# Weight sums of 41 of the 44 gate and value groups: accumulating DMAs in place of additions on VectorE and GpSimd

## The chip, the cores and the metric

One core of one Trainium2 chip runs the whole program. The core has a matrix engine (TensorE, PE in the profile, whose weight loads are the row PEld), VectorE (DVE), ScalarE (ACT), GpSimd (POOL) and SyncE (SP), and 16 DMA engines that move data between device memory (HBM) and on-chip memory (SBUF). Matmul results land in PSUM, which the DMA engines of this kernel never write. The metric is the device time of one execution in microseconds (us).

## The reference, cut to what matters

One decoder layer on 512 positions of width 2048: a hybrid of block-sparse attention and a state-space scan, an output projection, and a gated feed-forward block. The change lies in the feed-forward block:

```python
h = rms_norm(x, norm2_w)
u = causal_dwconv(h @ w_up, ffn_conv_w, ffn_conv_b)     # 2048 -> 2 * 5632, conv over 3 positions
u_gate, u_val = jnp.split(u, 2, axis=-1)
return x + (jax.nn.silu(u_gate) * u_val) @ w_down       # 5632 -> 2048
```

All arrays are float32. 5632 is 44 x 128, so there are 44 groups, each with 128 gate channels and the 128 value channels that belong to them.

## The kernel before

**Products.** Every matmul works on numbers split into a high and a low part (fp32r tiles `hi` and `lo`, ScalarE copies the high part, VectorE subtracts it to get the low part), and a product of two such numbers is three matmuls: hi x hi, hi x lo and lo x hi. The feed-forward products use a 2x2 block scheme with seven block products instead of eight, P1 to P7. A group's weights are four pieces of 128 x 1024 floats (512 KB each), named "11", "12", "21" and "22". Three of the seven products take a piece as it is (P1: 11, P2: 12, P4: 22, loaded a second time as "22b"); the other four take sums of pieces:

- T1 for P5: 21 and 22 added (`add` step s1, VectorE, line 1034)
- T2 for P6: T1 with 11 subtracted (s2, VectorE, line 1038)
- T4 for P3: 12 with T2 subtracted (s4, VectorE, line 1040)
- T3 for P7: 11 with 21 subtracted (s3, GpSimd, line 1027)

T1, T2 and T4 follow one another in place in one tile, the chain (`s`, in PSUM, two buffers). T3 is made in place in the tile that holds 21 (`rawb`, two buffers). The other pieces go into `rawa` (four buffers). The activations are combined in the same manner once (`sums`), and the results of the seven products are combined by `up_after` (first phase, "up", 44 groups) or `down_after` (second phase, "down", 24 groups in three passes of 7, 8 and 7 k-blocks).

**Order.** `items` is the list of products. Group g takes seven slots in the order P5(g), P3(g-1), P1(g), P4(g-1), P6(g), P2(g), P7(g). In the up phase an item is 24 matmuls of 128 x 256. Everything else hangs on slots: `at(slot, fn)` puts a step before or (`where=after`) after the low-part split of a slot, so the order on each engine is written out by hand. At slot k the kernel emits the matmuls of item k, then what reads their result, then the low part of item k+2 (`split_lo`, line 1060, two `lo2` buffers) and the high part of item k+3 (`split`, line 1051, three `hi2` buffers). ScalarE and VectorE work their queues in order; SP works the loads in order.

**Special items.** In groups 1, 2, 4, 15 and 30, and in three groups of each down pass, P3 is multiplied in another order and against a second copy of one activation tile (`twin`, line 1309). The result is the same.

**Ends of the phase.** The up phase starts when the output projection's last columns (`g_x2`) have been summed, and the scale 1/rms (`rstd`, a power on GpSimd at slot 3, transposed on TensorE at slot 4) is made during its first slots. From the last up group on, VectorE and ScalarE also split the gated activations that come back from HBM (`b_split`, lines 1106 and 1107) for the down phase. The gated activations of two up groups are collected in one tile `gt` and written by one DMA (line 1067, `gd<-gt`).

Of the kernel before, what the change touches and what calls it, by code (L numbers as in the profile page):

```python
# [20 lines left out]
F32 = mybir.dt.float32  # L21
# [3 lines left out]
OP = mybir.AluOpType  # L25
# [162 lines left out]
def body(ctx, tc, xT, wi, wz, wo, wu, wd0, wd1, wd2, pp, pf, outT, dbg={}):  # L188
# [697 lines left out]
    def sums(E, g, part=None):  # L886

        if part != 1:
            E.tensor_tensor(g[:, 4:6, :], g[:, 1:4:2, :], g[:, 0:2, :], op=OP.subtract)
        if part != 0:  # L890
            E.tensor_tensor(g[:, 6, :], g[:, 3, :], g[:, 4, :], op=OP.subtract)
            E.tensor_tensor(g[:, 7, :], g[:, 2, :], g[:, 6, :], op=OP.subtract)
# [121 lines left out]

    def load(gi, name):
        if name == "21":
            r = lp.tile([128, 1024], F32, name="rawb", bufs=2)
        else:
            r = lp.tile([128, 1024], F32, name="rawa", bufs=4)
        sy.dma_start(r[:, :cols(gi)], groups[gi]["src"][name[:2]])  # L1020
        raw[gi, name] = r

    def add(gi, name):
        n = cols(gi)
        if name == "s3":
            r = raw[gi, "21"][:, :n]
            po.tensor_tensor(r, raw[gi, "11"][:, :n], r, op=OP.subtract)  # L1027
            return
# [8 lines left out]
        if name == "s2":  # L1037
            ve.tensor_tensor(s_, s_, raw[gi, "11"][:, :n], op=OP.subtract)
        else:
            ve.tensor_tensor(s_, raw[gi, "12"][:, :n], s_, op=OP.subtract)  # L1040
# [28 lines left out]
    for gi in range(len(groups)):  # L1069
        p5, p1 = pos[gi, "P5"], pos[gi, "P1"]  # L1070
        p6 = pos[gi, "P6"]
        at(p5 - 8, load, gi, "21"), at(p5 - 8, load, gi, "22")
        at(p1 - 7, load, gi, "11"), at(pos[gi, "P2"] - 7, load, gi, "12"), at(pos[gi, "P4"] - 6, load, gi, "22b")
        if gi:
# [89 lines left out]
    def down_after(g, x):  # L1164
# [3 lines left out]
                              "P7": (X[:, lo], 1, hi, OP.add), "P4": (X[:, lo], 1, lo, OP.add),  # L1168
                              "P5": (X[:, hi], 1, hi, OP.add), "P3": (X[:, hi], 0, hi, OP.add),
# [3 lines left out]
        ve.tensor_tensor(a[:, row, half], src, a[:, row, half], op=op)  # L1173
# [9 lines left out]
    def up_after(g, x):  # L1183
# [9 lines left out]
        elif x == "P3":  # L1193
            ve.tensor_tensor(ug[:, 258:514], X[:, 256:], g["P6"], op=OP.add)
        else:
            ve.tensor_tensor(uv[:, 2:258], X[:, :256], rbc[:, :256], op=OP.mult)
            up_side(i, ug, uv)

    def up_side(i, ug, uv):
# [28 lines left out]
        for d, fn in ((0, lambda: ve.tensor_tensor(ug[:, 2:514], ug[:, 2:514], rbc, op=OP.mult)),  # L1228
                      (1, lambda: ve.tensor_tensor(uv[:, 258:514], uv[:, 258:514], rbc[:, 256:], op=OP.mult)),
# [119 lines left out]
```

## Time and profile before

| what | value |
|---|---|
| time, median of 2 runs | 2087.6 us (2086.79 to 2088.41) |
| span of the profiled execution, first to last instruction | 2086.9 us |
| profiled execution's time by the page | its span; the median run is 0.7 us above it |
| TensorE busy over the span | 98% |
| VectorE, ScalarE, GpSimd busy | 76%, 48%, 10% |
| DMA traffic | 328.18 MB, mean 157 GB/s |
| up phase | about 780 us to 1615 us |

A row of the windows view gives, for a stretch of time, each engine's busy time and instruction count, the granted TensorE clock, the mean busy share of the 16 DMA engines and the rate at which they moved bytes. A row of the groups by line gives the source line, the engine, the operation, result and operands, the form, the count, then total busy time and the mean in nanoseconds of one. A row of the timeline gives start, duration, engine, line, and in brackets how long the engine had idled and what released it. A row of the waits gives total, count and longest.

### The profile page before, as it was taken

To read this page: it belongs to the slowest core of one execution; us is meant where nothing else is said; L and a number is where in the kernel's file an instruction comes from. 1 tells how busy PE (TensorE), PEld (TensorE's weight loads), DVE (VectorE), ACT (ScalarE), POOL (GpSimd) and SP (SyncE) were. 2 spreads that over 40 slices of the span, in tenths; PEclk is the share of its full clock that TensorE was granted. 3 is DMA by queue.
4 is the path that set the end of the run, shared out by engine and by line. 5 is a ranking of instruction groups with operands and counts; after the bars stand their busy time and mean duration, and the time that the engine had idled before them with its cause. 6 is when DMAs were issued, how large, how long until landed. Compare 5 with 4: busy or idle time off the path is not lost.

```text
span 2086.9 us, 37696 instructions
## 1 busy us (share of the span) xinstructions
PE 2048.4 (98%) x15366; PEld 1934.0 (93%) x15366; DVE 1581.2 (76%) x2251; ACT 994.9 (48%) x1437; POOL 208.1 (10%) x107
## 2 busy tenths in 40 slices
PE   9999999999999998999999999999999899999999
PEld 8888888888888878999999999999999799899999
DVE  6545555345565557999999999999999977977976
ACT  6433435244445435555555555555555634534533
POOL 0020000000000001111110111011101111101110
PEclk9999999999999999999999999999999999999999
DMA  5233222332225545445444544454446667856763
GB/s 196 76 114 95 71 73 80 97 106 81 82 71 166 165 142 188 160 143 192 162 159 165 172 172 163 151 192 152 156 178 212 208 220 243 276 186 234 264 202 122
DMA packets 114396, 328.18 MB, mean 157 GB/s; under 512 B 10736, under 2 KB 35120, under 8 KB 111408
## 3 DMA queue, kind: packets, MB, share of 16 engines
q1 hardware_dynamic: 114224, 325.78, 46.4%
q8 instruction: 120, 1.97, 0.4%
q14 instruction: 52, 0.43, 0.1%
HBM read 283.77 MB, written 41.98 MB: 156 GB/s over the span
## 4 chain that ended last, share of the span: by engine, by line
PE 90%; DVE 6%; issue 1%; DMA 1%; ACT 1%; SPq 0%; DVEq 0%; POOL 0%; ACTq 0%; POOLq 0%
PE acc L183 30%; PE x L1320 15%; PE x L1317 15%; PE x L1318 15%; PE sm L183 4%; PE y L1317 3%; PE y L1320 3%; PE y L1318 3%; PE x L1309 2%; DVE lo L1060 2%; DVE cmb L1107 1%; DVE acc L1173 0%; DMA ld<-gd 0%; DVE s L1034 0%; DVE lo L183 0%
## 5 line engine op out<-in xcount | busy, mean ns | idle before, releaser
L1317 PE MATMUL x<-cmb,hi 128*128 128x256 f32 x3062 | 720.4, 278 | 12.4 <-ACT cP L1188 5.4
L1318 PE MATMUL x<-cmb,hi 128*128 128x256 f32 x3062 | 720.4, 278 | 11.6 <-DVE cmb L1107 11.6
L1317 PEld LDWEIGHTS x<-cmb,hi 128*128 128x128 f32 x3062 | 577.3, 189 | 14.9 <-issue 8.4
L1318 PEld LDWEIGHTS x<-cmb,hi 128*128 128x128 f32 x3062 | 577.4, 189 | 14.4 <-DVE cmb L1107 14.2
L1320 PE MATMUL x<-cmb,lo 128*128 128x256 f32 x3062 | 414.3, 277 | 1.0 <-DVE lo L1060 0.9
L1320 PEld LDWEIGHTS x<-cmb,lo 128*128 128x128 f32 x3062 | 379.0, 189 | 1.8 <-DVE lo L1060 1.8
L183 DVE TENSOR_TENSOR lo<-raw,hi 128x512 fp32r<-128x512 f32 (+1 forms) x240 | 164.4, 691 | 234.6 <-ACT hi L183 218.4
L1051 ACT ACTIVATE hi<-s 128x1024 fp32r<-128x1024 f32 (+1 forms) x201 | 201.1, 1000 | 284.6 <-DVE s L1034 186.1
L1027 POOL TENSOR_TENSOR rawb<-rawa,rawb 128x1024 f32<-128x1024 f32 (+1 forms) x68 | 169.9, 2498 | 1288.1 <-DVE s L1034 1087.6
L183 PE MATMUL acc<-A,hi 128*128 128x512 f32 x704 | 279.2, 397 | 0.8 <-ACT hi L183 0.8
L183 PE MATMUL acc<-A,lo 128*128 128x512 f32 x704 | 275.4, 391 | 0.0
L183 PE MATMUL acc<-B,hi 128*128 128x512 f32 x704 | 274.9, 391 | 0.0
L183 ACT ACTIVATE hi<-raw 128x512 fp32r<-128x512 f32 (+1 forms) x240 | 149.2, 629 | 247.5 <-PE acc L183 212.2
L1060 DVE TENSOR_TENSOR lo<-s,hi 128x1024 fp32r<-128x1024 f32 (+1 forms) x201 | 238.3, 1186 | 15.4 <-issue 13.2
L1060 DVE TENSOR_TENSOR lo<-rawa,hi 128x1024 fp32r<-128x1024 f32 (+1 forms) x204 | 241.5, 1184 | 4.2 <-PE x L1320 4.2
L1051 ACT ACTIVATE hi<-rawa 128x1024 fp32r<-128x1024 f32 (+1 forms) x204 | 209.6, 1028 | 37.1 <-PE x L1318 36.9
L183 PEld LDWEIGHTS acc<-A,lo 128*128 128x128 f32 x704 | 132.5, 188 | 28.8 <-DVE lo L183 0.6
L183 PEld LDWEIGHTS acc<-A,hi 128*128 128x128 f32 x704 | 132.9, 189 | 26.7 <-ACT hi L183 1.0
L183 PEld LDWEIGHTS acc<-B,hi 128*128 128x128 f32 x704 | 132.8, 189 | 26.0
L1188 ACT ACTIVATE cP<-x 128x256 f32<-128x256 f32 x132 | 50.7, 384 | 204.9 <-PE x L1320 204.9
L183 PE MATMUL acc<-hi,A 128*128 128x256 f32 (+2 forms) x448 | 134.6, 300 | 0.7 <-DVE u L183 0.7
L183 PE MATMUL acc<-hi,B 128*128 128x256 f32 (+2 forms) x448 | 132.7, 296 | 0.0
(211 smaller groups left out, 2865.2 us busy)
## 6 DMA issues: line engine op xcount, KB each, us to landing
rawa<-wu SPq DMA_DIRECT2D x176, 512.0 KB, 3.6
raw<-wi SPq DMA_DIRECT2D x79, 512.0 KB, 3.6
rawa<-wd SPq DMA_DIRECT2D x64, 448.0 KB, 4.3
rawb<-wu SPq DMA_DIRECT2D x44, 512.0 KB, 4.6
gd<-gt SPq DMA_DIRECT2D x22, 1024.0 KB, 4.5
raw<-wo SPq DMA_DIRECT2D x32, 512.0 KB, 3.5
rawa<-wd SPq DMA_DIRECT2D x32, 512.0 KB, 4.5
ld<-gd SPq DMA_DIRECT2D x27, 512.0 KB, 6.4
```

Of the source, the lines that this page charges most:

```text
L183: return fn(out, *args, **kw)
L1027: po.tensor_tensor(r, raw[gi, "11"][:, :n], r, op=OP.subtract)
L1051: se.activation(h[:, :n], src[:, :n], AF.Copy)
L1060: ve.tensor_tensor(l[:, :n], src[:, :n], h[:, :n].bitcast(F32), op=OP.subtract)
L1107: ve.tensor_tensor(lo, ld[:, :m, :], hi.bitcast(F32), op=OP.subtract)
L1188: se.activation(g[x], X[:, 256:] if x == "P5" else X[:, :256], AF.Copy)
L1309: pe.matmul(out, a[:, q * 128:(q + 1) * 128], b[:, q, :], start=False, stop=last and q == n - 1, skip_group_check=True)
L1317: pe.matmul(out, w, bk[:, 0, q, :], start=fresh and q == 0, stop=False, skip_group_check=True)
L1318: pe.matmul(out, w, bk[:, 1, q, :], start=False, stop=False, skip_group_check=True)
L1320: pe.matmul(out, l[:, q * 128:(q + 1) * 128], bk[:, 0, q, :], start=False, stop=q == n - 1, skip_group_check=True)
```

## The change

For groups 1 to 41 (`by_dma`) none of the four sums is made by an engine any more. SP loads 21 into the chain, and GpSimd issues a DMA that reads 22 from HBM and adds it to what is in the chain (`accum_op=OP.add`): that is T1. The same way 11 is added to the chain for T2 and 12 for T4. For T3, SP loads 21 a second time, into `rawb`, and GpSimd's DMA adds 11 to it. The chain of these groups lies in SBUF (`acc_s`, two buffers), since a DMA is to write it. Groups 0, 42 and 43 and the down phase keep the additions on VectorE and GpSimd.

An accumulating DMA adds, so all sums have to be additions. With 21 and 22 taken with turned sign, every subtraction of the scheme becomes an addition; the turned sign is carried by the activation sums (`sums`: three of the four outputs are formed in another way, two of them with a scalar-tensor-tensor instruction) and taken out of the results (`down_after` subtracts three products, `up_after` and `up_side` multiply the value half by -1 along with the scale).

```diff
         if part != 1:
-            E.tensor_tensor(g[:, 4:6, :], g[:, 1:4:2, :], g[:, 0:2, :], op=OP.subtract)
+            E.tensor_tensor(g[:, 4:6, :], g[:, 0:4:3, :], g[:, 1:2, :].to_broadcast([128, 2, 256]), op=OP.subtract)
         if part != 0:
-            E.tensor_tensor(g[:, 6, :], g[:, 3, :], g[:, 4, :], op=OP.subtract)
-            E.tensor_tensor(g[:, 7, :], g[:, 2, :], g[:, 6, :], op=OP.subtract)
+            E.scalar_tensor_tensor(g[:, 6, :], g[:, 4, :], -1.0, g[:, 3, :], op0=OP.mult, op1=OP.subtract)
+            E.scalar_tensor_tensor(g[:, 7, :], g[:, 6, :], -1.0, g[:, 2, :], op0=OP.mult, op1=OP.subtract)
...
+    by_dma = lambda gi: 0 < gi < NF - 2
+
+    def summed(gi, name):
+
+        d = groups[gi]["src"]
+        if name == "t1":
+            chain[gi] = lp.tile([128, 1024], F32, name="acc_s", bufs=2)
+            sy.dma_start(chain[gi], d["21"])
+            po.dma_start(chain[gi], d["22"], accum_op=OP.add)
+        elif name == "t3":
+            raw[gi, "21"] = lp.tile([128, 1024], F32, name="rawb", bufs=2)
+            sy.dma_start(raw[gi, "21"], d["21"])
+            po.dma_start(raw[gi, "21"], d["11"], accum_op=OP.add)
+        else:
+            po.dma_start(chain[gi], d["11" if name == "t2" else "12"], accum_op=OP.add)
+
...
-        at(p5 - 8, load, gi, "21"), at(p5 - 8, load, gi, "22")
+        if by_dma(gi):
+            at(p5 - 8, summed, gi, "t1"), at(p5 - 3, summed, gi, "t3")
+            at(p5 - 2, summed, gi, "t2", where=after), at(p6 - 2, summed, gi, "t4", where=after)
+        else:
+            at(p5 - 8, load, gi, "21"), at(p5 - 8, load, gi, "22")
         at(p1 - 7, load, gi, "11"), at(pos[gi, "P2"] - 7, load, gi, "12"), at(pos[gi, "P4"] - 6, load, gi, "22b")
+        if by_dma(gi):
+            continue
...
-            ve.tensor_tensor(uv[:, 2:258], X[:, :256], rbc[:, :256], op=OP.mult)
+            ve.scalar_tensor_tensor(uv[:, 2:258], X[:, :256], -1.0, rbc[:, :256], op0=OP.mult, op1=OP.mult)
             up_side(i, ug, uv)
...
-                      (1, lambda: ve.tensor_tensor(uv[:, 258:514], uv[:, 258:514], rbc[:, 256:], op=OP.mult)),
+                      (1, lambda: ve.scalar_tensor_tensor(uv[:, 258:514], uv[:, 258:514], -1.0, rbc[:, 256:],
+                                                           op0=OP.mult, op1=OP.mult)),
```

How the queues change is seen best in what stands in them. First GpSimd's queue at the start of the up phase, before (`rawb_7072` is group 0, `rawb_7082` group 1, and so on; `rstd` is the scale):

```order
L183 TENSOR_TENSOR rk_5572<-rk_5572,nhalf_134 128x4
L1027 TENSOR_TENSOR rawb_7072<-rawa_7076,rawb_7072 128x1024
L1027 TENSOR_TENSOR rawb_7082<-rawa_7166,rawb_7082 128x1024
L183 TENSOR_TENSOR rstd_132<-rstd_132,nhalf_134 128x4
L1027 TENSOR_TENSOR rawb_7309<-rawa_7420,rawb_7309 128x1024
L1027 TENSOR_TENSOR rawb_7550<-rawa_7653,rawb_7550 128x1024
```

The same place in the changed kernel (`acc_s_7082` is the chain of group 1, `acc_s_7309` of group 2, `acc_s_7549` of group 3; line 1023 makes T1, line 1029 T2 and T4, line 1027 T3):

```order
L183 TENSOR_TENSOR rk_5572<-rk_5572,nhalf_134 128x4
L1023 DMA acc_s_7082<-wu 128x1024
L1043 TENSOR_TENSOR rawb_7072<-rawa_7076,rawb_7072 128x1024
L1027 DMA rawb_7230<-wu 128x1024
L183 TENSOR_TENSOR rstd_132<-rstd_132,nhalf_134 128x4
L1029 DMA acc_s_7082<-wu 128x1024
L1023 DMA acc_s_7309<-wu 128x1024
L1029 DMA acc_s_7082<-wu 128x1024
L1027 DMA rawb_7483<-wu 128x1024
L1029 DMA acc_s_7309<-wu 128x1024
L1023 DMA acc_s_7549<-wu 128x1024
L1029 DMA acc_s_7309<-wu 128x1024
```

One instruction a group has become four, and their steady order is T2 of a group, T1 of the next, T4 of the group, T3 of the next. Two of them now stand ahead of the power that makes `rstd`.

Second, VectorE's queue about the P5 of an up group in mid-phase, before (`s_8908` is the chain of the group that begins, `s_8672` that of the group that ends, `lo2` the low parts):

```order
L889 TENSOR_TENSOR gt_8608<-gt_8608 128x512
L1228 TENSOR_TENSOR ug0_7150<-ug0_7150,rbc_131 128x512
L1060 TENSOR_TENSOR lo2_8906<-rawb_8497,hi2_8876 128x1024
L1034 TENSOR_TENSOR s_8908<-rawb_8736,rawa_8738 128x1024
L1229 TENSOR_TENSOR uv0_7152<-uv0_7152,rbc_131 128x256
L1190 TENSOR_TENSOR ug1_7154<-y_8914,cP1_8837 128x256
L1040 TENSOR_TENSOR s_8672<-rawa_8705,s_8672 128x1024
L1060 TENSOR_TENSOR lo2_8943<-s_8908,hi2_8912 128x1024
L1192 TENSOR_TENSOR uv1_7156<-x_8747,cP5_8772 128x256
L1060 TENSOR_TENSOR lo2_8976<-s_8672,hi2_8945 128x1024
```

The same place in the changed kernel:

```order
L889 TENSOR_TENSOR gt_8602<-gt_8602 128x512
L1250 TENSOR_TENSOR ug0_7149<-ug0_7149,rbc_131 128x512
L1076 TENSOR_TENSOR lo2_8902<-rawb_8664,hi2_8869 128x1024
L1251 SCALAR_TENSOR_TENSOR uv0_7151<-uv0_7151,rbc_131 128x256
L1212 TENSOR_TENSOR ug1_7153<-y_8907,cP1_8829 128x256
L1076 TENSOR_TENSOR lo2_8935<-acc_s_8730,hi2_8905 128x1024
L1214 TENSOR_TENSOR uv1_7155<-x_8740,cP5_8765 128x256
L1076 TENSOR_TENSOR lo2_8968<-acc_s_8492,hi2_8938 128x1024
```

The two 128 x 1024 additions between the low parts are gone (a third, line 1038, is gone a few rows further on), and the low parts read the chain from SBUF. On SP a group has five loads as before, with one of 22 replaced by a second one of 21; the load into the chain has to wait until the low part of P3 of the group two before has been read out of that buffer.

More of the change, by code (lines that the diff above doesn't have):

```diff
@@ L1026, in add @@
             r = raw[gi, "21"][:, :n]
-            po.tensor_tensor(r, raw[gi, "11"][:, :n], r, op=OP.subtract)
+            po.tensor_tensor(r, raw[gi, "11"][:, :n], r, op=OP.add)
             return
@@ L1037, in add @@
         if name == "s2":
-            ve.tensor_tensor(s_, s_, raw[gi, "11"][:, :n], op=OP.subtract)
+            ve.tensor_tensor(s_, s_, raw[gi, "11"][:, :n], op=OP.add)
         else:
-            ve.tensor_tensor(s_, raw[gi, "12"][:, :n], s_, op=OP.subtract)
+            ve.tensor_tensor(s_, raw[gi, "12"][:, :n], s_, op=OP.add)
     SOURCE = {"P1": "11", "P2": "12", "P4": "22b", "P7": "21"}
@@ L1167, in down_after @@
         src, row, half, op = {"P1": (X[:, lo], 0, lo, OP.add), "P6": (X[:, lo], 0, hi, OP.add),
-                              "P7": (X[:, lo], 1, hi, OP.add), "P4": (X[:, lo], 1, lo, OP.add),
-                              "P5": (X[:, hi], 1, hi, OP.add), "P3": (X[:, hi], 0, hi, OP.add),
+                              "P7": (X[:, lo], 1, hi, OP.subtract), "P4": (X[:, lo], 1, lo, OP.subtract),
+                              "P5": (X[:, hi], 1, hi, OP.subtract), "P3": (X[:, hi], 0, hi, OP.add),
                               "P2": (g.get("Y"), 0, lo, OP.add)}[x]
@@ L1172, in down_after @@
             src = src[:, lo]
-        ve.tensor_tensor(a[:, row, half], src, a[:, row, half], op=op)
+        ve.tensor_tensor(a[:, row, half], a[:, row, half], src, op=op)
         if g is groups[-1]:
```

## The prediction

> **What bounds the kernel now.** I read the page's busy row first, then the windows by stage, then the waits.
>
> ```profile
> span 2086.9 us, 37696 instructions
> PE 2048.4 (98%) x15366; PEld 1934.0 (93%) x15366; DVE 1581.2 (76%) x2251; ACT 994.9 (48%) x1437; POOL 208.1 (10%) x107
> ```
> ```profile
> 780.00:790.00 10.00, 4.76 (x24) 4.48 (x24) 8.63 (x13) 4.19 (x9) 2.38 (x1) 0.76 0.75 265
> ...
> 800.00:1000.00 200.00, 200.00 (x1753) 200.00 (x1754) 186.33 (x229) 109.66 (x139) 27.69 (x12) 1.00 0.46 162
> 1000.00:1200.00 200.00, 200.00 (x1766) 200.00 (x1765) 189.30 (x236) 106.81 (x138) 24.65 (x10) 1.00 0.48 166
> ...
> 1400.00:1600.00 200.00, 200.00 (x1767) 200.00 (x1766) 190.07 (x239) 106.73 (x138) 24.64 (x10) 1.00 0.50 174
> 1600.00:1800.00 200.00, 184.68 (x1562) 180.82 (x1561) 173.97 (x222) 97.65 (x110) 27.34 (x11) 0.99 0.70 236
> ```
> ```profile
> POOL rawb L1027 <- DVE s L1034: 1087.6, 66, 21.7
> ...
> PE x L1318 <- DVE cmb L1107: 11.6, 13, 2.3
> ...
> PE x L1317 <- ACT cP L1188: 5.4, 2, 5.0
> ```
>
> TensorE is idle for 2086.9 - 2048.4 = 38.5 us in all, and for none of it between 800 and 1600 us, where groups 1 to 41 run. There VectorE is 93 to 95% busy (186.33 to 190.07 of 200), close behind but never waited for. What TensorE loses in the up and down phases lies at the start (5.2 us of 780:790) and at the handover to the down phase (15.3 us of 1600:1800), where it waits for the split of gated activations (`cmb`, line 1107). DMA is at half load (0.48, 166 GB/s in the second of these rows), GpSimd sits and waits.
>
> So the most any change could win without touching the matmuls is 38.5 us, 1.8% of the median. Differences of over 2% (41.8 us) are what a measurement of this kernel can surely tell from no change: faster by that much is out of reach here.
>
> **What the change removes.**
>
> ```profile
> L1034 DVE TENSOR_TENSOR s<-rawb,rawa 128x1024 f32<-128x1024 f32 x51 | 62.5, 1226 | 0.0
> L1038 DVE TENSOR_TENSOR s<-s,rawa 128x1024 f32<-128x1024 f32 x51 | 62.5, 1225 | 0.0
> L1040 DVE TENSOR_TENSOR s<-rawa,s 128x1024 f32<-128x1024 f32 x51 | 62.2, 1219 | 0.0
> L1027 POOL TENSOR_TENSOR rawb<-rawa,rawb 128x1024 f32<-128x1024 f32 x52 | 130.4, 2507 | 1030.7 <-DVE s L1034 847.1 <-DVE gx L183 183.6
> ```
>
> Per group VectorE loses 1.226 + 1.225 + 1.219 = 3.67 us, over 41 groups 150 us; GpSimd loses 41 x 2.507 = 103 us. All of it lies beside a TensorE that has no gap. On the path: 0. At the handover VectorE does bind, but groups 42 to 45, whose sums fall into it, keep their additions, so nothing is won there either, unless VectorE enters it with a backlog. It does not: with 5% idle just before (190.07 of 200), it is caught up.
>
> **The signs.** Two 256-column and, for each pair of groups, two more 256-column operations on VectorE become scalar-tensor-tensor.
>
> ```profile
> L1207 DVE SCALAR_TENSOR_TENSOR tg<-ug,par,tg 128x512 f32<-128x512 f32 x88 | 65.6, 745 | 0.8 <-ACT tg L1206 0.8
> ...
> L1218 DVE TENSOR_TENSOR gt<-tg,tv 128x512 f32<-128x512 f32 x44 | 30.4, 691 | 1.5
> ```
>
> That costs 745 - 691 = 54 ns at 512 columns, 27 to 54 ns at 256: at most 3 x 0.054 = 0.16 us a group, against 3.67 us freed. On the path only the two of the last activation sum before the up phase: 0.1 us.
>
> **What it adds: DMA bytes.** A group moved six 512 KB units: five loads and half of a 1 MB write of gated activations (166 GB/s x 19.04 us = 6.0 units; 19.04 us is the step between the last two PE rows but two below). Now it is six and four accumulating ones. What a unit costs under pressure I take from the busiest stretch with TensorE full:
>
> ```profile
> 1596.00:1604.00 8.00, 8.00 (x73) 8.00 (x72) 7.13 (x10) 3.05 (x5) 0.00 (x0) 1.00 1.08 369
> ```
>
> 369 GB/s makes 1.42 us a unit. No row shows an accumulating DMA; call its weight w units. Then the engines need (6 + 4w) x 1.42 us of every 19.04, which fits up to w = 1.85. From below w = 1, a plain load (14.2 us, 75%). From above I bound it at w = 3 (fetch, fetch again, write, with no overlap): 25.6 us, 6.5 us over, x 41 = 267 us. I take a value under 1.85, nearer to the plain load, since the bytes written are the same and the second operand comes from on-chip memory.
>
> The Trainium skill, page "Collectives: The Full Stack", section "The bandwidth ceiling: the fold count and why AG ≠ RS ≠ AR", speaks against that: an add in the DMA path needs two source reads, and a reducing transfer ran at 1/1.93 of a copying one. No run here has shown it yet; by w = 1.93 the engines' need would be 19.5 us, 0.44 over, 18 us in all.
>
> **What it adds: latency.** An addition was 1.2 us in the queue of the engine that needed it; now a DMA has to be issued and land between one use of the chain and the next.
>
> ```profile
> rawa<-wu SPq DMA_DIRECT2D x176, 512.0 KB, 3.6
> ...
> rawb<-wu SPq DMA_DIRECT2D x44, 512.0 KB, 4.6
> ...
> ld<-gd SPq DMA_DIRECT2D x27, 512.0 KB, 6.4
> ```
> ```profile
> 1016.09 1.22 DVE L1060 TENSOR_TENSOR lo<-s,hi 128x1024 fp32r<-128x1024 f32 x1
> 1017.68 1.22 DVE L1060 TENSOR_TENSOR lo<-s,hi 128x1024 fp32r<-128x1024 f32 x1
> ...
> 1025.56 1.23 DVE L1060 TENSOR_TENSOR lo<-s,hi 128x1024 fp32r<-128x1024 f32 x1
> ```
> ```profile
> 1023.86 1.01 ACT L1051 ACTIVATE hi<-s 128x1024 fp32r<-128x1024 f32 x1
> 1025.50 0.38 ACT L1188 ACTIVATE cP<-x 128x256 f32<-128x256 f32 x1 [0.64 <-PE x L1320]
> ```
> ```profile
> 1018.96 1.07 PE L1320 MATMUL x<-cmb,lo 128*128 128x256 f32 x8
> ...
> 1027.12 1.07 PE L1320 MATMUL x<-cmb,lo 128*128 128x256 f32 x8
> 1029.84 1.07 PE L1320 MATMUL x<-cmb,lo 128*128 128x256 f32 x8
> ...
> 1038.00 1.07 PE L1320 MATMUL x<-cmb,lo 128*128 128x256 f32 x8
> ```
>
> The PE rows are the last third of an item: P5 of a group at 1018.96, P4 of the one before at 1027.12, P6 at 1029.84, the next P5 at 1038.00; an item takes 2.72 us.
>
> T2: the low part of P5 is done at 1016.09 + 1.22 = 1017.3; P6 starts at about 1028.0 (27.12 + 0.9), and ScalarE needs 1.01 for its high part and 0.38 for the copy behind it, so the sum must be there by 1026.6. Window 9.3 us. ScalarE, in order, holds `cP` behind it, which P6 needs too; that is counted.
>
> T4: low part of P6 done at 1026.8, P3 of this group starts at 1038.9, needed by 1037.5: 10.7 us. T1 of the next group: its buffer is free when the low part of the old P3 is done (1018.9), the load of 21 lands by 1023.5 (4.6 us), needed before the P5 that starts at 1036.2, so by 1034.8: 11.3 us. T3 has a whole group's time more.
>
> An accumulating DMA behaves like a load of 3.6 us at best; at worst like two in a row of 6.4 us, 12.8 us. I take 6 to 8 us, one loaded transfer and part of a second. That fits into 9.3. On GpSimd's queue each waits only for its own chain; the T2 behind a T3 waits for a load issued some five items ahead.
>
> **Start and writes.** The power for `rstd` now stands behind T3 of group 1.
>
> ```profile
> 790.97 0.98 SPq L1020 DMA_DIRECT2D rawa<-wu  x2
> ```
> ```profile
> 802.42 1.92 POOL L183 TENSOR_TENSOR rstd<-rstd,nhalf 128x4 f32<-128x4 f32 x1 [1.29 <-DVE rstd L183]
> ```
>
> The second load of 21 follows those two, so by 792.4, lands by 798.8 even at 6.4 us, and leaves 3.6 us before the power was ready to run: 0. The write of `gt` has to leave its tile before the next pair's product:
>
> ```profile
> 1019.72 0.33 SPq L1067 DMA_DIRECT2D gd<-gt  x1
> ```
> ```profile
> 1027.48 0.69 DVE L1218 TENSOR_TENSOR gt<-tg,tv 128x512 f32<-128x512 f32 x1
> ```
>
> It has 7.8 us and needed 4.5 (median of the page for this write); with more traffic it may be late by a microsecond or two, which VectorE, 3.67 us a group lighter, can bear.
>
> **A small stall costs twice.** After its waits at the start TensorE ran its items slower, until the first special item:
>
> ```profile
> 819.66 1.10 PE L1320 MATMUL x<-cmb,lo 128*128 128x256 f32 x8
> 822.49 1.10 PE L1320 MATMUL y<-cmb,lo 128*128 128x256 f32 x8
> ```
>
> 2.83 us against 2.72, at a granted clock of 1.00. So one late sum in mid-phase may cost 7 x 0.11 = 0.77 us a group until the special item of group 15 or 30 or the end: about 7 groups on average, 5 us. I allow for half such a case, 2.5 us.
>
> **Sum.** 2086.9 + 0 + 0.1 + 2.5 + 0.7 (around the span) = 2090 us.
>
> **The rivals.**
>
> *Two reads, engines just full.* If an accumulate reads both its operands through the engine that loads read one through, w is 1.85 to 2.03 and the engines are barely overbooked: at 2.03, (6 + 4 x 2.03) x 1.42 - 19.04 = 1.0 us a group, so 2090 to 2129 us in all, still within 2%. For it: DMA runs at 0.48 with six units. Against: the 369 GB/s were reached by traffic with HBM, and half of the new reads are on-chip. It is the rule of the collectives page of the Trainium skill that is weighed above.
>
> *DMA is the bound* (w from 2.03 on). TensorE waits for every chain: 2130 to 2355 us, with w = 2.3 at (6 + 4 x 2.3) x 1.42 - 19.04 = 2.5 us a group 2192. For it: nobody's row shows how fast the adding is. Slower.
>
> *Late sums on GpSimd's queue.* If an accumulate takes more than 9.3 us from release to landing, or if the queue carries one at a time, the chain and not TensorE sets the pace. One at a time at 5.5 us each makes 22 us a group, 3 us over: x 41 = 121, so 2209; at 6.4 us 2357. It decides from 19.04 / 4 = 4.76 us per DMA. For it: GpSimd's queue has never issued a DMA in this trace. Against: nothing in the queue's order asks an accumulate to wait for the one ahead. The Trainium skill, page "SBUF — State Buffer", section "SBUF: two separate sides", adds that GpSimd cannot write descriptors while VectorE runs certain two-port operations; at 1.2 us an operation of VectorE this would lengthen each by about that, and not break the 9.3. Slower.
>
> *The handover gains.* A lighter VectorE and GpSimd give back part of the 15.3 us of 1600:1800: 2076 to 2084. Against: the additions that fall there stay.
>
> That the additions do not leave VectorE is no rival: the order above shows them gone.
>
> **Chances.** Hidden as forecast 0.43 (its own range 2084 to 2106); handover gains 0.04; engines just full 0.17; DMA the bound 0.19; late sums 0.17. Faster by over 2% 0.01 (no row allows it), within 2% 0.64, slower 0.35. The range reaches from the handover case to where half of the slower cases lie, 2080 to 2210.
>
> **What would show it.** Right: TensorE busy 200 of 200 in 1000:1200 and 1400:1600, VectorE near 153 of 200 there, DMA share 0.75 to 0.9, no wait of ScalarE's `hi<-acc_s` for a DMA of more than 2 us. Wrong by bandwidth: share at 1.0 and late plain loads too. Wrong by latency: share below 0.9 and ScalarE waiting for the accumulates alone. An item time of 2.83 in mid-phase would show the double cost.

## The result and the profile after

The changed kernel takes 2118.22 us (median of 2 runs, 2117.22 to 2119.23) against 2087.6: a ratio of 1.0149, 95% interval 1.0119 to 1.0178. The profiled execution's span is 2115.5 us, 28.6 above that of before. So it is slower, by less than 2%: inside the forecast's range, and 28 us above its number.

The busy row of the page of after, and two stretches of the windows view (columns: stretch, its length, busy time and instructions of PE, PEld, DVE, ACT, POOL, clock, DMA share, GB/s):

```profile
PE 2064.5 (98%) x15366; PEld 1943.7 (92%) x15366; DVE 1445.1 (68%) x2128; ACT 995.6 (47%) x1437; POOL 249.9 (12%) x230
```
```profile
1000.00:1200.00 200.00, 196.17 (x1674) 195.22 (x1674) 147.69 (x195) 101.11 (x130) 35.55 (x41) 1.00 0.98 264
...
1400.00:1600.00 200.00, 194.97 (x1700) 193.40 (x1700) 148.55 (x197) 101.60 (x131) 35.69 (x41) 1.00 0.99 267
```

TensorE now has gaps (3.8 and 5.0 us of 200) where it had none. It also did 1674 matmuls in a stretch in which it did 1766 before, 5% fewer, although it was busy for only 2% less: the matmuls became slower too. VectorE is as light as it was meant to be. The DMA engines went from a share of 0.48 to 0.98.

The waits of after (total, count, longest), and the DMA issues of its page (KB each, median us from issue to landing):

```profile
ACT hi L1067 <- DMA acc_s<-wu: 199.8, 76, 5.4
...
DVE gt L1240 <- DMA gd<-gt: 17.0, 16, 2.2
...
PE x L1340 <- ACT hi L1067: 13.7, 20, 1.5
```
```profile
rawa<-wu SPq DMA_DIRECT2D x135, 512.0 KB, 7.5
acc_s<-wu POOLq DMA_DIRECT2D x123, 512.0 KB, 8.5
rawb<-wu SPq DMA_DIRECT2D x44, 512.0 KB, 8.4
gd<-gt SPq DMA_DIRECT2D x22, 1024.0 KB, 7.7
acc_s<-wu SPq DMA_DIRECT2D x41, 512.0 KB, 5.8
```

ScalarE waits for the chain (`acc_s`), TensorE for ScalarE. An accumulating DMA of the chain lands 8.5 us after its issue (median), and the plain loads beside it have gone from 3.6 to 7.5 and from 4.6 to 8.4.

**One stall in full.** The stalls come about every 40 us, once for two groups, one or two at a time. Rows of the timeline of after, from SP, GpSimd, ScalarE and VectorE, in order of time:

```profile
1063.71 1.23 DVE L1076 TENSOR_TENSOR lo<-acc_s,hi 128x1024 fp32r<-128x1024 f32 x1 [1.01 <-ACT hi L1067]
...
1064.96 0.33 SPq L1022 DMA_DIRECT2D acc_s<-wu  x1
1065.76 0.33 SPq L1083 DMA_DIRECT2D gd<-gt  x1
1066.14 1.75 SPq L1036 DMA_DIRECT2D rawa<-wu  x2
1067.94 1.02 SPq L1026 DMA_DIRECT2D rawb<-wu  x1
1069.69 0.33 SPq L1036 DMA_DIRECT2D rawa<-wu  x1
...
1070.24 1.22 DVE L1076 TENSOR_TENSOR lo<-acc_s,hi 128x1024 fp32r<-128x1024 f32 x1
...
1071.53 0.86 POOL L1023 DMA_DIRECT2D acc_s<-wu  x1 [7.89 <-DVE lo L1076]
1072.13 1.17 POOL L1029 DMA_DIRECT2D acc_s<-wu  x1
...
1081.15 1.06 ACT L1067 ACTIVATE hi<-acc_s 128x1024 fp32r<-128x1024 f32 x1 [5.40 <-DMA acc_s<-wu]
...
1084.15 1.06 ACT L1067 ACTIVATE hi<-acc_s 128x1024 fp32r<-128x1024 f32 x1 [1.94 <-DMA acc_s<-wu]
```

At 1064.94 the old P3's low part frees the chain's buffer, and SP issues the load of 21 (line 1022). It lands 5.9 us after its issue. T1 (line 1023) goes out 0.7 us after that landing, as in every group between 840 and 1595 us (its row names VectorE's low part, which ended a moment before T1 but frees T4), and lands 9.5 us after its own issue: 16.1 in all. The prediction's own figures leave 15.9 for that path (4.6 for the load and 11.3 for T1). ScalarE stands idle for 5.4 us.

T4 (line 1029) is late too. Its chain is free at 1071.46, when P6's low part (the row at 1070.24) is done. It goes out at 1072.13, right behind T1, and lands 11.9 us later: 12.6 us after its release, where the prediction left 10.7. ScalarE waits another 1.94 us for it.

Behind the load of 21, which SP's queue had waited to issue, the 1 MB write of the activations and four plain loads go out within five microseconds.

### The profile page after: what moved, and what is told of

It is laid out like the page before. It is cut to its first block, busy times and chain, and to the rows that moved or that the text cites. A ratio compares the mean times of both kernels' runs of the same rounds, so it can differ in the third digit from the quotient of the medians.

```text
span 2115.5 us, 37850 instructions
## 1 busy us (share of the span) xinstructions
PE 2064.5 (98%) x15366; PEld 1943.7 (92%) x15366; DVE 1445.1 (68%) x2128; ACT 995.6 (47%) x1437; POOL 249.9 (12%) x230
## 4 chain that ended last, share of the span: by engine, by line
PE 62%; DMA 23%; DVE 9%; ACT 3%; issue 3%; POOL 1%; SPq 0%; POOLq 0%; ACTq 0%; DVEq 0%
PE acc L183 29%; DMA acc_s<-wu 21%; PE x L1340 8%; PE x L1341 8%; PE x L1343 8%; PE sm L183 4%; DVE lo L1076 4%; ACT hi L1067 2%; PE x L1332 1%; DVE cmb L1129 1%; PE y L1340 1%; PE y L1341 1%; PE y L1343 1%; DMA t<-xT 1%; DMA ld<-gd 1%
## 5 line engine op out<-in xcount | busy, mean ns | idle before, releaser
L1341 PE MATMUL x<-cmb,hi 128*128 128x256 f32 x3062 | 724.9, 279 | 10.2 <-DVE cmb L1129 10.2
L1076 DVE TENSOR_TENSOR lo<-acc_s,hi 128x1024 fp32r<-128x1024 f32 x126 | 154.3, 1225 | 134.7 <-ACT hi L1067 126.0
L1067 ACT ACTIVATE hi<-acc_s 128x1024 fp32r<-128x1024 f32 x126 | 133.2, 1057 | 230.8 <-DMA acc_s<-wu 199.8
L1067 ACT ACTIVATE hi<-rawa 128x1024 fp32r<-128x1024 f32 (+1 forms) x204 | 209.4, 1027 | 37.4 <-PE x L1341 37.2
L1067 ACT ACTIVATE hi<-s 128x896 fp32r<-128x896 f32 (+1 forms) x78 | 75.0, 961 | 165.4 <-DVE s L1050 100.9
L183 PE MATMUL acc<-lo,A 128*128 128x256 f32 (+2 forms) x448 | 132.7, 296 | 0.0
```

Of the source, the lines that this page charges most:

```text
L183: return fn(out, *args, **kw)
L1067: se.activation(h[:, :n], src[:, :n], AF.Copy)
L1076: ve.tensor_tensor(l[:, :n], src[:, :n], h[:, :n].bitcast(F32), op=OP.subtract)
L1341: pe.matmul(out, w, bk[:, 1, q, :], start=False, stop=False, skip_group_check=True)
```

## The experiments

All runs were timed against the kernel before on the same chip. Besides the median, the table gives what the items of the profiled execution took between 830 and 1600 us, worked out from the starts of the last row of each item (24 matmuls): items at about 2.83 us instead of 2.72, and items that are later than that (stalls), each with the time above 2.72 that they add up to.

| run | median, us | ratio (95%) | DMA share 1000:1200 | items at 2.83 | stalls |
|---|---|---|---|---|---|
| before | 2087.6 | 1 | 0.48 | 0 | 0 |
| changed | 2118.2 | 1.0149 (1.0119 to 1.0178) | 0.98 | 73 (7.9 us) | 25 (22.4 us) |
| 1 plain DMAs | 2087.9 | 0.9995 (0.9985 to 1.0004) | 0.77 | 0 | 0 |
| 2 three buffers | 2088.8 | 1.0004 (0.9995 to 1.0013) | 1.01 | 0 | 0 |
| 3 more special items | 2126.5 | 1.0182 (1.0161 to 1.0204) | 0.98 | 4 (0.6) | 35 (34.0) |
| 4 T4 on VectorE | 2111.8 | 1.0109 (1.0094 to 1.0124) | 0.87 | 44 (4.9) | 13 (10.3) |
| 5 signs alone | 2088.9 | 1.0000 (0.9991 to 1.0010) | 0.47 | 0 | 0 |
| 6 three buffers, groups 1 to 43 | 2107.2 | 1.0089 (1.0074 to 1.0105) | 1.00 | 0 | 0 |
| 7 T1 on VectorE | 2170.7 | 1.0394 (1.0378 to 1.0409) | 0.82 | 33 (3.6) | 36 (67.3) |
| 8 write cut in two | 2107.3 | 1.0084 (1.0068 to 1.0101) | 1.00 | 161 (17.2) | 11 (8.8) |
| 9 as 8, more special items | 2101.7 | 1.0065 (1.0049 to 1.0082) | 1.01 | 3 (0.5) | 14 (9.2) |
| 10 as 7, T3 behind T2 | 2089.0 | 1.0000 (0.9990 to 1.0009) | 0.92 | 0 | 0 |
| 11 load of 21 on GpSimd | 2138.5 | 1.0242 (1.0221 to 1.0263) | 0.98 | 61 (6.7) | 32 (40.7) |
| 12 T3 behind T2, all four | 2194.0 | 1.0511 (1.0486 to 1.0537) | 0.90 | 48 (5.6) | 66 (90.8) |

For the changed kernel 7.9 + 22.4 = 30.3 us, about the 28.6 us between the two spans and 1.9 us by which its up phase is ahead at the start (group 1's special item ends at 829.1 us and not at 831.0).

The order of the products in the trace says which sum each of the changed kernel's 25 stalls waits for. Twelve stand at P5, which takes T1 (12.4 us), and 13 at P3, which takes T4 (10.0 us); none stands at P6, which takes T2. All lie in the groups in which the write of the activations goes out beside the load of 21. In these the load with T1 takes 15.6 us in the median, from the load's issue to T1's landing, in the others 13.4. T2 lands after 5.5 us in the median, T1 after 8.6, and T4, issued 0.6 to 2.4 us behind T1, after 10.2 (up to 12.2). From its release T4 takes more than its 10.7 us in 18 of 38 groups.

The theories at the outset: the DMA engines are full (bandwidth); the chain's sums take longer, from release to landing, than the two buffers leave (the chain); and a stall costs mostly by the slower items behind it.

**1. The same DMAs without the adding**

```diff
-            po.dma_start(chain[gi], d["22"], accum_op=OP.add)
+            po.dma_start(chain[gi], d["22"])
```

and so with the other two lines that accumulate. The adding is left out, so that the sums are not formed; queues, order and transfers stay.

> The 164 DMAs on GpSimd's queue stay where they are, with the same waits and bytes written, but copy instead of adding (the adding is left out, so the sums are not formed). Bandwidth theory (an accumulate takes twice the engine time of a copy: 2.79 against 1.40 us per 512 KB in the changed kernel): need falls from 6 x 1.40 + 4 x 2.79 = 19.6 to 10 x 1.4 = 14 us per 19.04, DMA share about 0.75, no TensorE gap in mid-phase, 2086 to 2092 us. Queue theory (issue and completion on GpSimd's queue are what is slow): landing stays near 8.5 us, TensorE still stalls every second group, 2110 us or more.

Windows row, and the DMA queues in the same stretch (packets, MB, share): GpSimd's queue, q0, in this run, and then both queues in the changed kernel:

```profile
1000.00:1200.00 200.00, 200.00 (x1766) 200.00 (x1765) 156.35 (x206) 106.90 (x137) 22.82 (x43) 1.00 0.77 281
```
```profile
q0 software_dynamic: 6029, 21.98, 30.6%
```
```profile
q0 software_dynamic: 5772, 21.02, 56.0%
q1 hardware_dynamic: 7914, 31.44, 42.0%
```

All the loss is gone, and the copies into the chain land after 5.2 us (page). So it is not GpSimd's queue as such, nor the order of the waits, nor the chain's place in SBUF. The rows also give the price: in 200 us the accumulates' 21.02 MB are 40.1 units of 512 KB, and 0.56 x 200 / 40.1 is 2.79 us of all 16 engines each. A plain unit is 0.42 x 200 / 60.0 = 1.40 us in the changed kernel, and 1.46 us on GpSimd's queue here. An accumulate weighs w = 1.9 to 2.0 plain units.

**2. Three buffers for the chain**

```diff
-            chain[gi] = lp.tile([128, 1024], F32, name="acc_s", bufs=2)
+            chain[gi] = lp.tile([128, 1024], F32, name="acc_s", bufs=3)
```

and so at the three other places that name `acc_s`.

> Three chain buffers in place of two: the load of 21 no longer waits for the P3 of the group two before, the bytes and accumulates are the same. Bandwidth theory (the engines' time is used up, 0.98 to 0.99): the start of T1 moves forward but the need of 19.6 us per 19.04 stays, so 2105 to 2118 us and a share of 0.98. Chain theory (21's load, then T1, one after the other, do not fit between the release of the buffer and P5: 6.5 + 9.6 us in a window of 16): the stalls every second group go, 2086 to 2095 us, at a share of 0.95 to 1.

Windows row and queues of this run:

```profile
1000.00:1200.00 200.00, 200.00 (x1766) 200.00 (x1766) 155.26 (x206) 106.23 (x138) 35.86 (x41) 1.00 1.01 278
```
```profile
q0 software_dynamic: 6095, 22.15, 58.3%
q1 hardware_dynamic: 8376, 33.15, 42.1%
```

The bytes are the same, the share is 1.01, the accumulates still take 8.4 us (page), and TensorE has no gap. A share of 1.0 is therefore not by itself a bound here. The work does just fit: per group 6 x 1.33 + 4 x 2.76 = 19.0 us by these rows (0.421 x 200 / 63.2 and 0.583 x 200 / 42.2), in a step of 19.04. So bandwidth as the bound falls. The third buffer changes two things. The load of 21 with T1 no longer waits for the old P3: it now takes 21.8 us in the median, against 14.4 in the changed kernel, and costs nothing, since it starts so much earlier. And T1 goes out 7.7 to 10.4 us ahead of T4, not 0.6 to 2.4. T4 then lands after 8.5 us in the median instead of 10.2, and in every group within its 10.7 us from release (10.6 at most). T2 has the window that it had. So what overruns with two buffers is the load of 21 with T1, and T4 behind it; this run doesn't part the two.

**3. A special P3 item in every up group**

```diff
-        if x == "P3" and (gi in (1, 2, 4, 15, 30) or gi >= NF and g["m"] in (1, 2, 4)):
+        if x == "P3" and (0 < gi < NF or gi >= NF and g["m"] in (1, 2, 4)):
```

> The special P3 item (second copy of an activation tile, other order) in all up groups from 1 on, not only 1, 2, 4, 15 and 30. Theory that a stall leaves TensorE in a slower rhythm (2.83 us an item) until a special item comes: about 75 slow items x 0.11 = 8 us come back, less 0.07 us for each of 36 added special items (2.5 us): 2110 to 2114 us, and hardly any run of 2.83 longer than a group. Rival, that the 2.83 us are the load of the DMA engines or of SBUF itself: no change or slower, 2118 to 2122 us.

The items at 2.83 us are gone (73 to 4), and the time has risen: 35 stalls of 34.0 us together instead of 25 of 22.4. Both branches of the expectation missed. Where the chain sets the pace, faster items only reach the next late sum earlier; the slow rhythm cost nothing that this run could win back.

**4. T4 back on VectorE**

```diff
-            at(p5 - 2, summed, gi, "t2", where=after), at(p6 - 2, summed, gi, "t4", where=after)
+            at(p5 - 2, summed, gi, "t2", where=after), at(pos[gi, "P3"] - 3, add, gi, "s4")
```

> T4 goes back to VectorE (one addition of 1.2 us a group, chain in SBUF), T1, T2, T3 stay accumulating: three accumulates a group. Bandwidth theory: 6 x 1.40 + 3 x 2.79 = 16.8 us of 19.04, share about 0.88, stalls gone, 2086 to 2093 us. Chain theory (T1 behind 21's load): the same serial path, but each step lands earlier with fewer bytes in flight; 2088 to 2105 us.

At a share of 0.87 it is still 1.1% late, above both branches, which speaks against bandwidth again. By product, the stalls at P3, which takes T4, are all gone. Those at P5 (T1) stay, with 7.7 us instead of 12.4, and P6 (T2) has new ones, 2.5 us. So T4's lateness was a loss of its own, and T1's remains without it. Rows of the timeline (ScalarE, GpSimd twice, ScalarE):

```profile
1038.06 2.01 ACT L1067 ACTIVATE hi<-acc_s 128x1024 fp32r<-128x1024 f32 x2 [3.95 <-DVE acc_s L1056]
1039.12 0.89 POOL L1027 DMA_DIRECT2D rawb<-wu  x1 [9.29 <-DMA rawb<-wu]
1040.79 0.88 POOL L1029 DMA_DIRECT2D acc_s<-wu  x1 [0.78 <-DVE uv L1214]
...
1049.69 1.06 ACT L1067 ACTIVATE hi<-acc_s 128x1024 fp32r<-128x1024 f32 x1 [4.72 <-DMA acc_s<-wu]
```

The first row is P5's split and P3's, and it names s4, P3's addition on VectorE, as what ended the wait of 3.95 us. But P5's split needs T1, and T1 landed at 1037.98, 9.0 us after its issue. In every group between 840 and 1595 us P5's split starts 0.08 us after T1's landing, in most of them before s4 has run, so it was T1 that was waited for. T2 (line 1029), issued 1.7 us behind T3 (line 1027), takes 8.9 us.

**5. The signs alone**

```diff
-    by_dma = lambda gi: 0 < gi < NF - 2
+    by_dma = lambda gi: False
```

> Only the turned signs are kept: every group's sums stay on VectorE and GpSimd, as additions. If the signs cost what the prediction gave them (0.1 us on the path), this is 2087.7 us, 1.000 of before. If the stalls came from VectorE's longer operations and not from the DMAs, it would be near the changed kernel's 2118 us, with TensorE under 200 of 200 between 800 and 1600 us.

2088.86 against 2088.71 us: with an interval of about 2 us either way, the turned signs cost nothing that can be measured.

**6. Three buffers, and groups 42 and 43 by DMA**

```diff
-    by_dma = lambda gi: 0 < gi < NF - 2
+    by_dma = lambda gi: 0 < gi < NF
```

on top of run 2.

> Three buffers for the chain instead of two, as in the second run, and the sums of the last two up groups (42 and 43) by accumulating DMAs too. If VectorE's additions are what holds the handover to the down phase, the 15 us that TensorE is idle in 1600:1800 shrink by up to six additions of 1.2 us, 7 us: 2080 to 2085 us. If the handover waits for something else, or the new DMAs collide with its loads of gated activations, it is 2088 us or later.

Windows rows of the handover:

```profile
1600.00:1620.00 20.00, 17.26 (x136) 16.87 (x134) 8.80 (x12) 4.43 (x6) 0.00 (x0) 0.91 0.63 203
1620.00:1640.00 20.00, 9.14 (x56) 8.95 (x57) 8.29 (x11) 7.17 (x10) 2.65 (x3) 0.74 0.75 193
```

TensorE loses 13.6 us in these 40, with no other engine over 44% busy, and gains nothing behind them. The buffers `acc_s` also take the first loads of gated activations and the first accumulators of the down phase, so that the sums of 42 and 43 now share them with the handover. In these 40 us ScalarE waits 13.3 us for plain loads of weights (`rawa`) and 10.1 us for the chain. Which wait costs how much was not taken apart, so whether the handover before was waiting for these additions stays open: this run only shows that moving them in this way gains nothing.

**7. T1 on VectorE, T3 ahead of T2**

```diff
-            at(p5 - 8, summed, gi, "t1"), at(p5 - 3, summed, gi, "t3")
+            at(p5 - 8, load, gi, "21"), at(p5 - 8, load, gi, "22")
+            at(p5 - 3 if gi > 1 else 1, add, gi, "s1", where=after)
+            at(p5 - 3 if gi > 1 else 1, summed, gi, "t3", where=after)
```

with s1 writing into `acc_s`, and T3 adding to the 21 that s1 has read.

> Two buffers, and the first sum of each chain back on VectorE, written to the buffer by the addition itself; T2, T3 and T4 stay with the DMAs. Three accumulating DMAs a group and the same bytes as in the run with T4 on VectorE (2111.8 us). If it is the chain that sets the pace, and in it the load of 21 with T1 behind it (6.5 and 9.6 us one after the other in a window of 16), the stalls are gone: TensorE 199 to 200 of 200 between 1000 and 1600 us, 2087 to 2091 us. If it is the number of accumulating DMAs, or T2 and T4 are late too, it is as late as that run, 2105 to 2115 us.

Both branches missed: it is much later than either. Where it loses stands in the timeline (GpSimd twice, ScalarE):

```profile
1011.41 0.88 POOL L1025 DMA_DIRECT2D rawb<-wu  x1 [4.87 <-DVE uv L1251]
1013.83 0.88 POOL L1027 DMA_DIRECT2D acc_s<-wu  x1 [1.53 <-DVE uv L1214]
...
1023.54 1.06 ACT L1065 ACTIVATE hi<-acc_s 128x1024 fp32r<-128x1024 f32 x1 [5.38 <-DMA acc_s<-wu]
```

T3 (line 1025) waits for s1, and so always goes out 2.4 us ahead of T2 (1027). T2 then lands after 9.7 us (median; 7.9 to 12.1), and from its release it takes more than its window of 9.3 in 25 of 36 groups. Of the 67.3 us of stalls, 60.4 stand at P6, which takes T2.

**8. The write of the activations cut in two**

```diff
-                at(t0 + (11 if i < NF - 1 else 9), sy.dma_start, gd[p][:, pr - PASSES[p][0]], box["gt"])
+                at(t0 + (11 if i < NF - 1 else 9), sy.dma_start, gd[p][:, pr - PASSES[p][0], 4:8], box["gt"][:, 4:8, :])
+            else:
...
+                at(t0 + 8, sy.dma_start, gd[p][:, pr - PASSES[p][0], 0:4], box["gt"][:, 0:4, :])
```

> Two buffers and all four sums by DMA, but the 1 MB write of a pair's gated activations is cut into two of 512 KB, the first of them three items earlier, so that only half of it goes out beside the load of 21 and T1. If that write is what makes every second group's T1 late, the loss per pair of 1.8 us falls to under half: 2090 to 2105 us. If the chain is late without it, or all the bytes together are too many, nothing changes: 2114 to 2122 us.

The stalls fall from 22.4 to 8.8 us, to under half as expected, with all bytes left: those at P5 from 12.4 to 4.6 us, those at P3 from 10.0 to 4.2. So the write beside them is a large part of what makes T1 and T4 late in every second group. But the time falls by only 11 us, to just above the first branch, since 161 items now run at 2.83 us, 17.2 us together. Rows of TensorE, last third of two items:

```profile
1036.06 1.10 PE L1347 MATMUL x<-cmb,lo 128*128 128x256 f32 x8
1038.89 1.10 PE L1347 MATMUL y<-cmb,lo 128*128 128x256 f32 x8
```

**9. Run 8 with special items**, with the one-line edit of run 3.

> The kernel with the cut write (2107.3 us) left TensorE almost without gaps, but 161 of its 301 items between 800 and 1640 us took 2.83 us instead of 2.72, 17.7 us together. Here it gets a special P3 item in every up group, 36 more of about 0.07 us each (2.5 us). If a small late sum costs mainly by the slower items behind it, until the next special item, this is 2090 to 2096 us. If the slower items only fill time in which the chain would have been waited for anyway, as in the third run, it is 2107 to 2112 us.

2101.7 us lies between the two branches. In the profiled executions the items at 2.83 fall from 161 to 3 and the stalls stay (8.8 and 9.2 us), and the span falls from 2111.2 to 2098.1, about what the items say (17.2 - 0.5, less 36 special items of 0.07 = 2.5, is 14.2). By the medians it is 5.6 us, since the runs of kernel 8 spread over 9 us (2103.7 to 2113.1). The intervals of the two ratios overlap, so by the medians alone the gain isn't clear of noise. By the profiled executions the slow rhythm does cost time when the chain is late only now and then, and nothing when it is late all the time (run 3).

**10. Run 7 with T3 behind T2**

```diff
-            at(p5 - 3 if gi > 1 else 1, summed, gi, "t3", where=after)
...
-            at(p5 - 2, summed, gi, "t2", where=after), at(p6 - 2, summed, gi, "t4", where=after)
+            at(p5 - 2, summed, gi, "t2", where=after), at(p5 - 2, summed, gi, "t3", where=after), at(p6 - 2, summed, gi, "t4", where=after)
```

> The run with T1 on VectorE again (2170.7 us), but with T3 behind T2 on GpSimd's queue instead of 2.4 us ahead of it. There T2 took 9.7 us to land with T3 ahead. If it was this neighbour that made T2 late, and T1's path is the only one that the changed kernel overruns, this is 2087 to 2095 us, TensorE 198 to 200 of 200 between 1000 and 1600 us. If an addition on VectorE into the chain's buffer, or three accumulating DMAs a group as such, make the chain late, it stays above 2130 us.

Windows row, and the same three instructions, of this run:

```profile
1000.00:1200.00 200.00, 200.00 (x1766) 200.00 (x1765) 167.43 (x215) 107.34 (x139) 29.04 (x33) 1.00 0.92 249
```
```profile
1036.85 0.88 POOL L1027 DMA_DIRECT2D acc_s<-wu  x1 [8.12 <-DVE lo L1074]
1037.46 1.19 POOL L1025 DMA_DIRECT2D rawb<-wu  x1
...
1042.63 1.07 ACT L1065 ACTIVATE hi<-acc_s 128x1024 fp32r<-128x1024 f32 x1 [0.25 <-DMA acc_s<-wu]
```

The swap of two neighbours on GpSimd's queue is worth 82 us. T2 now takes 5.8 us in these rows, and T3, behind it, 9.1 (median of the page; 8.1 in run 7), for which it has time. With two buffers and three accumulates a group there is no gap left, once the serial path of load and T1 is gone and T2 has no neighbour ahead. T4, without a T1 just ahead of it, lands within 7.4 us.

A neighbour ahead isn't enough by itself to make T2 late, though. In the changed kernel T3 goes out 1.9 to 2.7 us ahead of T2 in six groups, and T2 lands after 5.6 to 6.4 us there. What else in run 7 adds to it was not taken apart.

**11. The load of 21 on GpSimd's queue**

```diff
-            sy.dma_start(chain[gi], d["21"])
+            po.dma_start(chain[gi], d["21"])
```

> The changed kernel with one line altered: the plain load of 21 into the chain's buffer is issued by GpSimd, ahead of T1, and not by SP. In the changed kernel SP's queue waits 489.5 us in 39 waits at that load for its buffer, and the write of the activations and four plain loads go out within 5 us behind it, beside it. If that burst is what makes the load of 21 (6.5 us) and T1 (9.6 us) overrun their 16 us, the other loads now go out earlier and apart, and the stalls are gone or nearly: 2088 to 2096 us. If T1 is late by T4, which GpSimd issues within a microsecond or two of it, or by the load of the DMA engines as a whole, or if the wait now holds up T4 on GpSimd's queue, it is 2112 us or more.

Later, not earlier. Timeline rows (GpSimd twice, ScalarE; GpSimd, SP twice, GpSimd twice, ScalarE) and a wait of SP:

```profile
1055.25 0.55 POOL L1022 DMA_DIRECT2D acc_s<-wu  x1 [1.92 <-DVE lo L1076]
1061.20 0.85 POOL L1023 DMA_DIRECT2D acc_s<-wu  x1 [5.39 <-DMA acc_s<-wu]
1067.12 1.06 ACT L1067 ACTIVATE hi<-acc_s 128x1024 fp32r<-128x1024 f32 x1 [1.84 <-DMA acc_s<-wu]
...
1072.38 0.55 POOL L1022 DMA_DIRECT2D acc_s<-wu  x1 [1.67 <-DVE gt L891]
1072.83 0.33 SPq L1083 DMA_DIRECT2D gd<-gt  x1
1073.25 2.39 SPq L1036 DMA_DIRECT2D rawa<-wu  x2
1080.52 0.85 POOL L1023 DMA_DIRECT2D acc_s<-wu  x1 [7.59 <-DMA acc_s<-wu]
1081.12 1.14 POOL L1029 DMA_DIRECT2D acc_s<-wu  x1
1088.71 1.06 ACT L1067 ACTIVATE hi<-acc_s 128x1024 fp32r<-128x1024 f32 x1 [4.40 <-DMA acc_s<-wu]
```
```profile
SPq L1083 <- DVE gt L892: 284.7, 22, 15.5
```

The burst was not broken up: SP's queue now waits at the write instead (284.7 us in 22 waits), and the write and the loads behind it again go out beside the load of 21. In these rows the first group has no write beside the load, the second has one. Over the groups between 840 and 1595 us the load of 21 lands after 4.0 us in the median without a write beside it (19 groups) and after 7.0 with one (18); T1 takes 8.2 and 8.6, hardly different (the 5.9 us in the first of these groups is the shortest of all). So it is the load that the write delays. T4 (1081.12) is also held behind T1 for a microsecond or so, as the second branch had it. Whether an SP queue without the burst would have cured the changed kernel was not shown.

**12. The changed kernel with T3 behind T2**

```diff
-            po.dma_start(raw[gi, "21"], d["11"], accum_op=OP.add)
+        elif name == "t3sum":
+            po.dma_start(raw[gi, "21"], d["11"], accum_op=OP.add)
...
-            at(p5 - 2, summed, gi, "t2", where=after), at(p6 - 2, summed, gi, "t4", where=after)
+            at(p5 - 2, summed, gi, "t2", where=after), at(p5 - 2, summed, gi, "t3sum", where=after), at(p6 - 2, summed, gi, "t4", where=after)
```

> The changed kernel with two buffers and all four accumulating DMAs, T3 moved behind T2 on GpSimd's queue. In the changed kernel T3 goes out 2 to 8 us after T1 and T4, beside their second half (T1 at 1071.5, T4 at 1072.1, T3 at 1079.9 us); behind T2 it falls into the 9 us in which T2 was alone. If the neighbours on the queue set how long T1 takes, as with T2 and T3 in the runs with T1 on VectorE, T1 lands in 8 us instead of 9.6 and most stalls go: 2088 to 2105 us, TensorE over 198 of 200 between 1000 and 1600 us. If it is the load of 21 with the burst of plain loads beside it, or T1 and T4 by themselves, the time stays at 2112 to 2122 us; if T2 suffers from T3 behind it, it is later still.

My expectation missed by 90 us. What cures run 7 is poison here (GpSimd twice, SP, GpSimd, ScalarE):

```profile
1040.99 0.88 POOL L1030 DMA_DIRECT2D acc_s<-wu  x1 [8.69 <-DVE uv L1215]
1041.59 1.18 POOL L1028 DMA_DIRECT2D rawb<-wu  x1
...
1043.09 0.33 SPq L1022 DMA_DIRECT2D acc_s<-wu  x1
...
1051.73 0.86 POOL L1023 DMA_DIRECT2D acc_s<-wu  x1 [8.96 <-DMA acc_s<-wu]
...
1060.38 1.06 ACT L1068 ACTIVATE hi<-acc_s 128x1024 fp32r<-128x1024 f32 x1 [6.18 <-DMA acc_s<-wu]
```

T3 now runs beside the load of 21, and T1 goes out 8.6 us after that load's issue instead of 6.6: 17.3 us in these rows for a path that has 15.9. P5 stalls in 32 groups and not in 12, which makes 55.8 of the 90.8 us; T2 is as quick as before (5.4 us in the median). The rest stands at P2 (21 us), P3 (10) and P7 (4) and was not taken apart. With a share of 0.90 it is the slowest of all, and run 2 with a share of 1.01 among the fastest.

## Why the prediction was right, and where it was not

The forecast of no change by over 2%, and of no gain, held. Its mechanism, that everything stays hidden, did not: 2118 us lies outside that case's own range (2084 to 2106), and its signs failed. TensorE was busy for 196.17 and 194.97 us instead of 200, the DMA share was 0.98 and 0.99 instead of 0.75 to 0.9, and ScalarE waited up to 5.4 us for a DMA instead of 2. The result lies in the full range of 2080 to 2210 because that range also covers the slower rivals. That the late sums cost 1.5% and stay within the 2% is luck: the sum holds 2.5 us for one late sum, where the medians lie 30.6 us apart.

- **No gain is possible.** Right. VectorE lost 3.2 of the 3.67 us a group (189.30 of 200 before, 155.26 in run 2, where TensorE is full as well), and no run was clearly faster than before. GpSimd did not get lighter: its additions went, but its issues took more (208.1 us busy before, 249.9 after). Moving the sums of 42 and 43 as well gained nothing at the handover (run 6).
- **The signs, 0.1 us.** Nothing that run 5 could measure, within about 2 us.
- **The write of `gt`, late by a microsecond or two, which VectorE bears.** Right: VectorE waits 17.0 us in 16 waits, the longest 2.2, and run 2 has no gap for it. What the term missed is whom the write delays: the load of 21 beside it (run 11: 7.0 us against 4.0), and so T1 and T4 (run 8).
- **DMA need.** The step "I take a value under 1.85, nearer to the plain load" failed: w measures 1.9 to 2.0. The limit was off as well: a plain unit under full load costs 1.33 to 1.40 us, not 1.42, so that even w = 2.0 fits with nothing to spare (run 2). The rule weighed there, of the Trainium skill's page "Collectives: The Full Stack", section "The bandwidth ceiling: the fold count and why AG ≠ RS ≠ AR", with its ratio of 1.93, agrees with the price that the runs show; the 18 us that I worked out by it did not follow, since full engines did not stop TensorE.
- **The rival "two reads, engines just full".** Its time (2090 to 2129) holds the result, and by its formula w = 2.0 gives (6 + 8) x 1.42 - 19.04 = 0.84 us a group, 34 us in all, near the 30.6 of the medians. It would have been the right number for the wrong reason: run 2 moves the same bytes in the time of before, and runs 4, 7 and 12 are late at shares of 0.82 to 0.90.
- **Latency: this is where the 28 us came from.** Two sizes were wrong. "I take 6 to 8 us" for an accumulating DMA was 8.5 us over the chain's sums, and by sum 5.5 for T2, 8.6 for T1 and 10.2 for T4 (medians). "The load of 21 lands by 1023.5 (4.6 us)" was 6.1 us in the median beside a write, and T1 goes out another 0.7 us later. The windows themselves hold up: T2's 9.3 us is kept at 5.8 us and overrun at 9.7 (runs 10 and 7), T1's 15.9 us overrun at 16.1 and 17.3 (changed kernel and run 12), T4's 10.7 us overrun at 12.6 (changed kernel) and kept in run 2. But I gave T1's path the load's time from a DMA system at half load and did not put the write and the loads queued behind it into the same stretch. I weighed bandwidth and latency as separate cases, but the runs show them together: plain loads landed after 3.6 and 4.6 us at a share of 0.48 and after 7.5 and 8.4 at 0.98.
- **"On GpSimd's queue each waits only for its own chain."** This step failed too. What stands just ahead matters: for T2 between 5.8 and 9.7 us (runs 10 and 7), for T4 between 8.5 and 10.2 (run 2 and the changed kernel, where T1 stands right ahead of it, as the printed order of the queue had shown). The rival "late sums on GpSimd's queue" had the right place, an accumulate that outlasts its window, with prices of 120 us and more. It came at 30 us, for T1 and T4 in every second group.
- **"A small stall costs twice."** Right in kind, allowed for at 2.5 us and seen at 7.9 (73 items). But it is no sum of its own while the chain sets the pace (run 3); it is most of the loss in run 8.
- **What would show it.** "Share at 1.0 and late plain loads too" was to mean bandwidth. Both signs were there, and the cause was another. What told them apart was run 2, which moves the same bytes with one buffer more and has no gap.

## What to carry to other kernels

When work moves from an engine to a DMA, lay out each path from the release of its buffer to the first use, with every transfer that is issued in that stretch, and take landing times for the load that the change itself creates: a buffer more made this change free, while one accumulate fewer alone did not (run 4). The order of two neighbouring DMAs on a queue was worth 82 us here (run 10), while the additions that they replaced cost nothing on the path; put the one with the short window first, and look at what the one behind it then runs into. A DMA share of 1.01 went with slow landings in run 2 (8.4 us) and bound nothing: look for the wait before you call it a bound.

## What the runs showed of the hardware

- An accumulating DMA from HBM into SBUF took 2.79 us of all 16 engines per 512 KB, a plain one on the same queue 1.46 us (changed kernel and run 1): 1.9 times as much, though one of the two operands lies on the chip.
- Of two accumulates of 512 KB that GpSimd issued 0.6 to 2.4 us apart, the second landed later: after 9.1 us behind one of 5.4 (run 10), 9.7 behind 8.1 (run 7) and 10.2 behind 8.6 (T4 behind T1 in the changed kernel), all medians. An accumulate 1.9 to 2.7 us behind another also landed after 5.6 to 6.4 us (T2 of the changed kernel, six groups), so the spacing alone doesn't say it.
- A 512 KB load landed after 4.0 us in the median, and after 7.0 us with a 1 MB write and its followers beside it (run 11).
- The issue of the same load of 21 held GpSimd for 0.55 us (run 11) and SP for 0.33 (changed kernel), though other issues of SP in the rows above took up to 1.02. An accumulate's issue held GpSimd for about 0.87. Answer on the tile `acc_s` of the changed kernel, durations in ns as minimum, median and maximum:

```profile
L1029 POOL DMA_DIRECT2D acc_s<-wu x20: 862/868/1175, 1002.7 to 1191.4; - x20
```

- The Trainium skill, page "SBUF — State Buffer", section "SBUF: two separate sides", says that certain two-port operations of VectorE hold up the writing of descriptors on GpSimd. With VectorE 74% busy no issue in this row takes over 1.2 us, so that no long holding up is seen at the issue; whether the landing contains some of it no run here separates.
- After a stall TensorE ran its items in 2.83 us instead of 2.72 at a granted clock of 1.00, for dozens of items, until a special item or another stall ended it (run 8: 161 of 272).
